# A transformer trunk on one core: an attention group's second projection wave done one projection at a time and evicted straight from PSUM, and VectorE work in the down projection tied to later instructions

## The chip, the cores and the metric

The kernel runs on one core of a Trainium2 chip. The metric is the device time of one execution in microseconds. The times come from runs of the kernel and from one execution taken by the hardware profiler. In the text PE is TensorE (matmul), DVE is VectorE, ACT is ScalarE, POOL is GpSimd, and SP is the queue from which most transfers are issued.

## The reference

A bidirectional encoder trunk of two layers on a sequence of 1024 tokens of width 1024, all in float32. Each layer has a parallel mix of four attention groups and then a squared-ReLU MLP:

```
for l in range(2):
    h = rms_norm(x, norm1_g[l])
    proj = h @ w_in[l]                      # columns of groups a, b, c, d
    y_a = mla_mixer(...)                    # latent attention, 4 heads
    y_b = diff_mixer(b_q, b_k, b_v, ...)    # differential attention, 4 heads, two softmaxes each
    y_c = swa_mixer(...)                    # +-128 window with sinks
    y_d = na_mixer(...)                     # neighbourhood attention on a 64-wide grid
    mix = concatenate([rms_norm(y_a), y_b, rms_norm(y_c), rms_norm(y_d)])
    x = x + mix @ w_out[l]
    h = rms_norm(x, norm2_g[l])
    x = x + square(relu(h @ w_up[l])) @ w_down[l]
return rms_norm(x, final_norm_g)
```

Group b's q and k get rotary position factors; its v does not.

## The kernel before

**Products in parts.** Data lies transposed: 128 features by 1024 tokens in a tile. A float32 product is made of three passes (`passes`, lines 218 to 223): each operand is split into a rounded high part and the rest, the low part, and TensorE computes high x high, high x low and low x high into one PSUM bank of 128x512. So a projection of 128 columns is 2 halves of tokens x 8 blocks of features x 3 passes = 48 matmuls. For weights, `weights` (line 202) loads a tile of four 128x128 blocks into `ws` (2 buffers), ACT rounds it into `wh`, and POOL computes the low part `wl` (tag `w`, 3 buffers of each). `split` (line 191) does the two steps. Which engine makes a low part is an argument; for activations it is mostly DVE.

**The schedule.** The program is written in an order, and a planner at build time sorts each engine's instructions by its own timing model and by priority (the order written, with offsets by `high_priority`). Tiles of a pool share buffers by tag. In the MLP TensorE's order is the written one (`manual_schedule`), the other engines' orders are planned. `issue_after(ins)` queues every instruction written inside it that runs on the engine of `ins` behind `ins` on that engine; it orders the queue and waits for nothing else.

**Start of attention** (`attention`, from line 407). PSUM has eight banks here: `mm` 2, `tr` 2, `sb` 3, `pv` 1. Group b's projections come in two waves of three: Q, K and V of the first pair of heads (wave 0), then those of the second pair (wave 1). `several` (line 231) computes a wave in six banks (`sb`, `sb`; `sb`, `tr`; `tr`, `pv`), in two rounds c over the two halves of the features; in a round all three projections take turns, so each round needs three weight tiles at a time. At the start of the second round it calls `catch_up`, which writes whatever has been put off in `self.due`. After a wave, each bank is copied by ACT into a tile `p` (line 480), and an eviction works from there:

- `ev_rope` (line 621) for Q and K, per half of the tokens: one DVE multiplication by the table `tabc`, two half-height ones by `tabs`, into two `part` tiles (3 buffers), an addition, and `emit_parts`: ACT's high part and a low part, then two transfers to memory. The addition and the low part run on `self.eng`: DVE for wave 0, POOL for wave 1.
- `ev_plain` (line 637) for V: one DVE multiplication by `rb`, and then `to_values`: a turn by four TensorE transposes into a bank, ACT's high part, DVE's low part, a transfer. For wave 0 the turn is put off in `self.due` and uses a bank of `mm`; for wave 1 it is written at once and uses `tr`.

Then `weave` interleaves the attention of group b (`attn_b`: scores into `sb`, DVE's row extreme `nm` on line 855, ACT's exponential, transposes into `tr`, products into `pv`) with a filler: the latent projections and those of group d, each through `one` (line 427): a weight pair by `wtile`, per half a bank of `mm`, `product`, `catch_up`, eviction. `attn_b` reads q, k and v back from memory (tile `stack`).

**Down projection** (`mlp_down`, line 1456). It is a Strassen-like scheme of seven block products for each of four groups j. For a group, `op(o)` loads four tiles of activations and splits them (ACT high, DVE low, tile `far`); `block` makes twelve matmuls of 128x512 with one raw weight tile, of which ACT and POOL make the parts; `add` is a DVE addition of a bank to the residual `x`. DVE also forms weight sums (tile `raw`): `s1`, and differences into `a21` and `a11`. In the written order a group has: four blocks with `op(1)`; four with `op(2)`, with each of them that column's sums; then `op(6)` and its four blocks, `op(7)`, `op(4)`, `op(5)`, `op(3)`. For j = 0 the up projection's last steps are mixed in: `finish_up[0]` with the DVE instruction kept in `self.rectified`, and everything on DVE of the second four blocks stands behind that instruction.

Of the kernel before, what the change touches and what calls it, by code (L numbers as in the profile page):

```python
# [15 lines left out]
AF = mybir.ActivationFunctionType  # L16
# [128 lines left out]
class Trunk:  # L145
# [85 lines left out]
    def several(self, srcs, xs, banks, ahead=None):  # L231

        for c in range(2):
            if c:
                self.catch_up()
            ws = ahead if ahead and c == 0 else [self.weights(s[c]) for s in srcs]
            for k in range(4):
                for w, b in zip(ws, banks):
                    for n in range(2):
                        self.passes(b[n], w[k], xs[4 * c + k], slice(n * 512, n * 512 + 512),  # L240
                                    c == 0 and k == 0, c == 1 and k == 3)
# [165 lines left out]
    def attention(self, l):  # L407
# [43 lines left out]
        with ExitStack() as stack, ExitStack() as att:  # L451
            self.ap = att.enter_context(sbuf("att"))
            with self.banks(mm=2, tr=2, sb=3, pv=1):
                with sbuf("proj", "right") as self.pp:
                    first = [w_in(t) for t in self.WAVES[0]]
                    saved = d["x"]
                    ahead = self.first
                    if l:
                        saved = self.dram.tile([8, P, S], F, tag="saved", bufs=1, name="saved")
                        for k in range(8):  # L460
                            self.keep(saved[k], self.x[k])
                        ahead = None
                    xs = self.normed(self.g1[:, l], lambda n: self.big_tile(R, n))

                    def wave():
                        return [(self.bank(a), self.bank(b)) for a, b in (("sb", "sb"), ("sb", "tr"), ("tr", "pv"))]

                    banks = wave()
                    self.several(first, xs, banks, ahead)
                    acc = self.squares(self.x, self.ap, "p", self.NP)  # L470
                    with tc.high_priority(offset=200):
                        self.spread_here(rb, self.rstd_cols(acc, DM, self.ones[:, 0:1]))
                    tabs = self.table("32", rb, nc.vector)
                    self.eng = nc.vector
                    for t in range(2):
                        for ev, b in zip(evacs_b(t), banks):
                            raw = self.ptile()
                            for n in range(2):
                                sl = slice(n * 512, n * 512 + 512)
                                nc.scalar.activation(raw[:, sl], b[n], AF.Copy)  # L480
                                ev(n, raw[:, sl])
                        if t == 0:
                            banks = wave()
                            self.several([w_in(t) for t in self.WAVES[1]], xs, banks)
                        self.eng = nc.gpsimd

                    fill = chain(self.proj_latent(l, one, xs, rb, tabs, lat, krd, rows), proj_d())
                    self.weave(chain.from_iterable(self.attn_b(l, t, qb, kb, vb, y["b"]) for t in range(2)),
                               fill, self.RB, self.LB, every=self.EV[0])
                    self.tails.append(self.mix_b(mix, y["b"], self.gsub[:, l:l + 1]))  # L490
                    fill = chain(proj_c(), self.latent_up(l, lat, rows, qa, ka, va))
                    self.weave(self.attn_d(l, qd, kd, vd, y["d"]), fill, self.RD, self.LD, every=self.EV[1])
                gout = lambda n: self.gout[n][:, l]
                self.tails.append(self.mix_group(mix, 2, y["d"], gout("na")))
                wa = stack.enter_context(sbuf("wa", "right"))
                wo = stack.enter_context(sbuf("wo", "right"))
                sums, w_out = [], d["w_out"][l]

                def groups_bd():

                    for m in range(self.EARLY):
                        x = wo.tile([P, S], F, tag="sum", bufs=self.EARLY, name="sum")
                        self.load(x, saved[m])
                        sums.append(x)
                    for k in (0, 2):
                        xs = mix[k:k + 2]
                        while None in xs:
                            yield True
                            xs = mix[k:k + 2]
                        for m, x in enumerate(sums):  # L510
                            ws = self.weights(w_out[m, 0][:, k:k + 2])
                            for n in range(2):
                                ps = self.mm_ps()
                                self.product(ps, ws, xs, n)
                                sl = slice(n * 512, n * 512 + 512)
                                self.tt(x[:, sl], ps, x[:, sl], ALU.add)
                                yield True

                fill = groups_bd()
                self.weave(self.attn_c(l, qc, kc, vc, y["c"]), fill, self.RC, end=False, every=self.EV[2])  # L520
                self.tails.append(self.mix_group(mix, 4, y["c"], gout("swa")))
                self.weave(self.attn_a(l, qa, ka, krd, va, y["a"]), fill, self.RA, self.LA, every=self.EV[3])
                self.tails.append(self.mix_group(mix, 6, y["a"], gout("mla"), nc.vector))
# [932 lines left out]
    def mlp_down(self, l, acts):  # L1456
# [4 lines left out]
        with self.banks(u=4, p=4):  # L1461
            def add(m, n, ps):
                o = self.x[m][:, N[n]]
                return self.tt(o, ps, o, ALU.add)

            for j in range(4):
# [31 lines left out]
                for m in M:  # L1498
                    a21.append(w(m + 4, 0, "c"))
                    a22.append(w(m + 4, 1, "c"))  # L1500
                with ExitStack() as behind:
                    if j == 0:
                        behind.enter_context(tc.issue_after(self.rectified.ins))
                    for m in M:
                        ps = self.bank("p")
                        self.block(ps, a12[m], b)
                        add(m, 0, ps)
                        s1.append(self.raw_weights("b"))
                        self.tt(s1[m], a21[m], a22[m], ALU.add)
                        sub(a21[m], a11[m], a21[m])  # L1510
                        sub(a11[m], s1[m], a11[m])
                if j == 1:
                    with tc.issue_after(added.ins):
                        self.finish_up[1]()
                b = op(6)
                for m in M:
                    self.block(u[m], a11[m], b, start=False)
                    add(m, 1, u[m])
                b = op(7)
                for m in M:  # L1520
                    self.block(u[m], a21[m], b, start=False)
                    add(m + 4, 1, u[m])
                    sub(a12[m], a12[m], a11[m])
                b = op(4)
                for m in M:
                    self.block(u[m], a22[m], b, start=False)
                    add(m + 4, 0, u[m])
# [136 lines left out]
```

## Time and profile before

| what | before |
|---|---|
| median of 3 runs | 2643.9 us (2641.38 to 2647.65) |
| profiled execution, its own time | 2649.87 us |
| its span | 2648.1 us |
| mean granted TensorE clock | 0.975 |
| PE busy | 2524.9 us, 95% of the span |
| DVE busy | 1950.6 us, 74% |
| ACT busy | 1443.9 us, 55% |
| POOL busy | 1134.4 us, 43% |
| instructions | 37521 |

The profiled execution is 6 us, 0.2%, above the median of the runs; its own time is 1.8 us more than its span. A row of the trace has a start, a duration in us, the engine, the line, the operation, the tiles out<-in, the shape, and in brackets how long the engine stood idle before it and what released it. Matmuls overlap, so the distance between two starts, not the duration, is what one costs. A row of the waits has the total, the times and the longest. A row of a group has the count, then busy time in us and the mean in ns, then idle time before.

### The profile page before, as it was taken

How to read it: one execution, taken by the hardware profiler on the slowest of the kernel's cores; microseconds unless marked ns; L12 is line 12 of the kernel's file. 1: busy time of each engine (PE TensorE's matmuls, PEld its weight loads, DVE VectorE, ACT ScalarE, POOL GpSimd, SP SyncE). 2: the span in 40 equal slices, each digit the busy share in tenths (PEclk: the TensorE clock that was granted, in tenths of full speed). 3: DMA queues.
4: the chain of work that ended last, by engine and by line, in shares of the span. 5: the costliest groups of instructions: out<-in, count | busy, mean ns of one | idle time of the engine just before them, and what ended most of it. 6: DMA issues, size and time to landing. Idle time of an engine off the chain costs nothing.

```text
span 2648.1 us, 37521 instructions
## 1 busy us (share of the span) xinstructions
PE 2524.9 (95%) x12320; PEld 2097.0 (79%) x12320; DVE 1950.6 (74%) x3403; ACT 1443.9 (55%) x2612; POOL 1134.4 (43%) x800
## 2 busy tenths in 40 slices
PE   8899998999999998999998999889999999989998
PEld 7678887877788887888877788777877888878886
DVE  6687767784986668887558777778749866678776
ACT  4577766673644444444426777666735444444445
POOL 2565642301055555555415657332011555555544
PEclk9889999999999999999998999899999999999999
DMA  5634598321144456544244445963221544665431
GB/s 169 183 88 130 146 268 260 101 90 50 63 167 153 153 192 225 154 150 140 99 119 145 118 133 155 281 206 90 80 72 35 193 147 155 234 194 165 131 116 64
DMA packets 191539, 385.00 MB, mean 145 GB/s; under 512 B 23712, under 2 KB 34928, under 8 KB 191344
## 3 DMA queue, kind: packets, MB, share of 16 engines
q1 hardware_dynamic: 176976, 356.90, 43.9%
q10 hardware_dynamic: 14368, 25.70, 2.8%
q8 instruction: 98, 1.61, 0.2%
q14 instruction: 97, 0.79, 0.1%
HBM read 261.20 MB, written 121.32 MB: 144 GB/s over the span
## 4 chain that ended last, share of the span: by engine, by line
PE 74%; DVE 10%; DMA 6%; ACT 4%; issue 3%; POOL 2%; SPq 1%; DVEq 0%; POOLq 0%; ACTq 0%
PE u L221 9%; PE u L223 9%; PE u L222 8%; PE p L223 5%; PE p L221 5%; PE p L222 5%; PE mm L221 5%; PE mm L222 5%; PE mm L223 5%; PE sb L853 3%; PE tr L889 2%; DVE p L855 2%; DVE part L189 2%; DMA bias<-in_bias 2%; ACT p L858 1%
## 5 line engine op out<-in xcount | busy, mean ns | idle before, releaser
L189 POOL TENSOR_TENSOR wl<-raw,wh 128x512 fp32r<-128x512 f32 x424 | 611.9, 1444 | 688.9 <-ACT wh L195 671.4
L195 ACT ACTIVATE wh<-raw 128x512 fp32r<-128x512 f32 x448 | 282.2, 630 | 559.0 <-PE u L222 302.0
L189 POOL TENSOR_TENSOR wl<-ws,wh 128x512 fp32r<-128x512 f32 (+1 forms) x120 | 151.9, 1267 | 420.9 <-ACT wh L195 411.4
L223 PE MATMUL u<-far,wl 128*128 128x512 f32 x768 | 300.7, 392 | 12.7 <-POOL wl L189 12.7
L221 PE MATMUL u<-far,wh 128*128 128x512 f32 x768 | 300.2, 391 | 2.3 <-ACT ev L1292 2.3
L222 PE MATMUL u<-far,wh 128*128 128x512 f32 x768 | 300.2, 391 | 0.0
L189 DVE TENSOR_TENSOR raw<-raw 128x512 f32<-128x512 f32 x256 | 227.0, 892 | 80.8 <-DMA raw<-in_w_up 45.1
L189 DVE TENSOR_TENSOR ptl<-tr,pth 128x512 fp32r<-128x512 f32 (+2 forms) x384 | 238.8, 629 | 61.2 <-ACT pth L195 59.6
L858 ACT ACTIVATE p<-p,nm 128x1024 f32<-128x1024 f32 x192 | 220.4, 1148 | 78.2 <-DVE nm L855 76.1
L195 ACT ACTIVATE pth<-tr 128x512 fp32r<-128x512 f32 (+2 forms) x384 | 206.9, 548 | 100.5 <-PE tr L889 68.4
L223 PE MATMUL p<-far,wl 128*128 128x512 f32 (+1 forms) x648 | 251.2, 388 | 3.0 <-DVE wl L189 3.0
L221 PE MATMUL p<-far,wh 128*128 128x512 f32 (+1 forms) x648 | 251.2, 388 | 0.0
L222 PE MATMUL p<-far,wh 128*128 128x512 f32 (+1 forms) x648 | 250.8, 387 | 0.0
L853 PE MATMUL sb<-stack 96*128 96x512 f32 x640 | 220.0, 426 | 15.7 <-DVE nm L855 15.1
L189 DVE TENSOR_TENSOR far<-act,far 128x512 fp32r<-128x512 f32 x224 | 202.2, 933 | 14.9 <-ACT far L195 14.9
L189 POOL TENSOR_TENSOR p<-p 128x1024 f32<-128x1024 f32 x64 | 154.6, 2416 | 104.1 <-ACT p L941 97.7
L223 PEld LDWEIGHTS u<-far,wl 128*128 128x128 f32 x768 | 145.1, 189 | 43.7 <-POOL wl L189 13.6
L221 PEld LDWEIGHTS u<-far,wh 128*128 128x128 f32 x768 | 145.0, 189 | 33.2 <-ACT ev L1292 3.1
L222 PEld LDWEIGHTS u<-far,wh 128*128 128x128 f32 x768 | 144.9, 189 | 30.8 <-DVE far L189 0.8
L889 PE MATMUL tr<-ident,p 128*128 128x128 f32 x1024 | 162.1, 279 | 7.5 <-DVE ptl L189 6.2
L221 PE MATMUL mm<-xh,wh 128*128 128x512 f32 x416 | 165.9, 399 | 2.1 <-DVE part L189 1.9
L855 DVE CUSTOM_DVE_ANT_0 p<-sb,zero 128x512 f32<-128x512 f32 x192 | 129.2, 685 | 52.3 <-PE sb L853 17.3
(256 smaller groups left out, 6148.4 us busy)
## 6 DMA issues: line engine op xcount, KB each, us to landing
act<-acts SPq DMA_DIRECT2D x224, 256.0 KB, 2.8
raw<-in_w_up SPq DMA_DIRECT2D x128, 256.0 KB, 2.7
acts<-ev SPq DMA_DIRECT2D x128, 256.0 KB, 2.2
raw<-in_w_down SPq DMA_DIRECT2D x128, 256.0 KB, 2.7
acts<-ev ACTq DMA_DIRECT2D x96, 256.0 KB, 2.5
ws<-in_w_in SPq DMA_DIRECT2D x76, 256.0 KB, 2.7
rz<-drows SPq DMA_DIRECT2D x40, 256.0 KB, 3.6
stack<-kd SPq DMA_DIRECT2D x32, 256.0 KB, 5.6
```

What stands on the lines that cost most here:

```text
L189: return (eng or self.nc.vector).tensor_tensor(out=out, in0=a, in1=b, op=op)
L195: self.rounded = nc.scalar.activation(hi, src, AF.Copy)
L221: mm(ps, w[0], x[0][:, sl], start=start, stop=False)
L222: mm(ps, w[0], x[1][:, sl], start=False, stop=False)
L223: mm(ps, w[1], x[0][:, sl], start=False, stop=stop)
L853: self.nc.tensor.matmul(ps, q[:, qt * P:(qt + 1) * P], k[:, sl], start=i == 0, stop=i == len(passes) - 1)
L855: self.nc.vector.tensor_tensor_reduce(out=p[:, sl], in0=ps, in1=self.zero[:, 0:1].bitcast(F).broadcast_to([P, 512]), scale=-scale, scalar= ...
L858: self.nc.scalar.activation(p, p, AF.Exp, bias=nm[:, 1:2], scale=-1.0, accum_out=z)
L889: nc.tensor.transpose(t[:, k * 256 + i * P:k * 256 + (i + 1) * P], p[:, (j * 2 + k) * P:(j * 2 + k + 1) * P], self.ident)
```

## The change

In `several` the call of `catch_up` between the rounds goes. In `attention` the evictions of wave 0 read the banks themselves, with no ACT copy; then wave 1 is done as `one` does it, projection by projection: both weight tiles, then per half of the tokens a bank (`mm` for Q, `sb` for K, `mm` for V), the product, `catch_up` and the eviction from the bank.

In `mlp_down` `op(6)` is written ahead of the second four blocks instead of behind them, in all four groups j. For j = 0 its DVE work stands behind the last addition of the first four blocks (`added`), and so does the DVE work of columns 2 and 3 of the second four; that of columns 0 and 1 stays behind `self.rectified`. For j = 0 the DVE work of `op(7)` and `op(4)` stands behind the last addition of the second four blocks (`passed`).

```diff
     def several(self, srcs, xs, banks, ahead=None):
 
         for c in range(2):
-            if c:
-                self.catch_up()
             ws = ahead if ahead and c == 0 else [self.weights(s[c]) for s in srcs]
...
                     self.eng = nc.vector
-                    for t in range(2):
-                        for ev, b in zip(evacs_b(t), banks):
-                            raw = self.ptile()
-                            for n in range(2):
-                                sl = slice(n * 512, n * 512 + 512)
-                                nc.scalar.activation(raw[:, sl], b[n], AF.Copy)
-                                ev(n, raw[:, sl])
-                        if t == 0:
-                            banks = wave()
-                            self.several([w_in(t) for t in self.WAVES[1]], xs, banks)
-                        self.eng = nc.gpsimd
+                    for ev, b in zip(evacs_b(0), banks):
+                        for n in range(2):
+                            ev(n, b[n])
+                    self.eng = nc.gpsimd
+                    for t, ev, tag in zip(self.WAVES[1], evacs_b(1), ("mm", "sb", "mm")):
+                        ws = self.wtile(w_in(t))
+                        for n in range(2):
+                            ps = self.bank(tag)
+                            self.product(ps, ws, xs, n)
+                            self.catch_up()
+                            ev(n, ps)
...
-                with ExitStack() as behind:
-                    if j == 0:
-                        behind.enter_context(tc.issue_after(self.rectified.ins))
-                    for m in M:
+                behind = lambda ins: tc.issue_after(ins.ins) if j == 0 else ExitStack()
+                c = b
+                with behind(added):
+                    b = op(6)
+                for m in M:
+                    with behind(self.rectified if m < 2 else added):
                         ps = self.bank("p")
-                        self.block(ps, a12[m], b)
-                        add(m, 0, ps)
+                        self.block(ps, a12[m], c)
+                        passed = add(m, 0, ps)
                         s1.append(self.raw_weights("b"))
                         self.tt(s1[m], a21[m], a22[m], ALU.add)
                         sub(a21[m], a11[m], a21[m])
...
-                b = op(6)
                 for m in M:
                     self.block(u[m], a11[m], b, start=False)
                     add(m, 1, u[m])
-                b = op(7)
+                with behind(passed):
+                    b = op(7)
                 for m in M:
                     self.block(u[m], a21[m], b, start=False)
                     add(m + 4, 1, u[m])
                     sub(a12[m], a12[m], a11[m])
-                b = op(4)
+                with behind(passed):
+                    b = op(4)
                 for m in M:
                     self.block(u[m], a22[m], b, start=False)
                     add(m + 4, 0, u[m])
```

## The prediction, made before the run

> **What bounds the kernel now.** I read the page's busy times first, then TensorE's waits stage by stage, and last the rows in order of time around the two places that the diff touches.
>
> ```profile
> span 2648.1 us, 37521 instructions
> PE 2524.9 (95%) x12320; PEld 2097.0 (79%) x12320; DVE 1950.6 (74%) x3403; ACT 1443.9 (55%) x2612; POOL 1134.4 (43%) x800
> ```
>
> TensorE is the bound, and the diff neither adds nor removes a matmul. So the change is worth what it takes from, or adds to, the time in which TensorE stands still or runs slowly. TensorE's waits, in the windows 0 to 130, 1000 to 1330, 1340 to 1470 and 2290 to 2649 us:
>
> ```profile
> PE sb L853 <- DVE nm L855: 5.3, 2, 3.0
> ...
> PE u L223 <- POOL wl L189: 6.1, 1, 6.1
> ...
> PE sb L853 <- DVE nm L855: 4.4, 2, 3.3
> PE tr L221 <- ACT wh L195: 3.9, 1, 3.9
> ...
> PE u L223 <- POOL wl L189: 6.7, 1, 6.7
> ```
>
> The start of each layer's attention and the start of each layer's down projection each hold a few long stalls; the 6.1 is the only wait of the down projection of layer 0 that the answer lists. Layer 0's attention start, in TensorE's order of time:
>
> ```profile
> 45.71 0.39 PE L221 MATMUL sb<-xh,wh 128*128 128x512 f32 x1
> 62.04 1.03 PE L679 MATMUL mm<-ident,part 128*128 128x128 f32 x8
> 68.38 0.39 PE L223 MATMUL tr<-xh,wl 128*128 128x512 f32 x1
> 72.18 0.50 PE L221 MATMUL tr<-xh,wh 128*128 128x512 f32 x1 [3.40 <-ACT wh L195]
> 73.04 0.63 PE L222 MATMUL pv<-xl,wh 128*128 128x512 f32 x1
> 75.60 0.63 PE L221 MATMUL tr<-xh,wh 128*128 128x512 f32 x1
> 84.38 0.39 PE L223 MATMUL pv<-xh,wl 128*128 128x512 f32 x1
> 97.03 0.39 PE L223 MATMUL mm<-xh,wl 128*128 128x512 f32 x1
> 113.54 0.63 PE L221 MATMUL mm<-xh,wh 128*128 128x512 f32 x1
> 116.52 0.63 PE L222 MATMUL mm<-xl,wh 128*128 128x512 f32 x1
> ```
>
> Wave 1 runs from 45.71 to 84.38. Its first 72 matmuls take 16.33 us, 0.227 each. There are two losses. **The weight switch:** nothing starts between 68.38 and 72.18 (3.6 us beyond one step), and then 7 matmuls step by 0.427 instead of 0.227 (73.04 to 75.60 is six steps), 1.4 us more: 5.0 us. **After the wave:** the latent projection's two halves end at 97.03 and its next product starts at 113.54. In those 16.3 us TensorE has this to do:
>
> ```profile
> L853 PE MATMUL sb<-stack 96*128 96x512 f32 x9 | 6.1, 733 | 5.5 <-DVE nm L855 5.3
> L679 PE MATMUL tr<-ident,part 128*128 128x128 f32 x8 | 2.2, 431 | 1.2 <-DVE part L189 1.2
> ```
>
> Nine 512-column scores at 0.23 are 2.1 us; the transposes and some single-column sums add about 1.1: 3.2 us of work, 13.1 lost, and 8 slow steps from 113.54 add 1.6: 14.7 us. VectorE at the same place:
>
> ```profile
> 43.85 3.42 DVE L189 TENSOR_TENSOR part<-p,tabs 64x512 f32<-64x512 f32 x2
> 58.88 1.29 DVE L189 TENSOR_TENSOR part<-p,rb 128x512 f32<-128x512 f32 x2
> 64.86 0.69 DVE L189 TENSOR_TENSOR both<-mm,both 128x512 fp32r<-128x512 f32 x1 [0.81 <-ACT both L683]
> 82.04 0.69 DVE L189 TENSOR_TENSOR part<-p,tabc 128x512 f32<-128x512 f32 x1 [16.49 <-ACT p L480]
> ...
> 107.92 0.68 DVE L189 TENSOR_TENSOR part<-mm,rb 128x512 f32<-128x512 f32 x1
> ```
>
> VectorE stands idle for 16.5 us while TensorE works through wave 1, because all six of the wave's banks finish together. Then the whole eviction of wave 1 meets the first softmaxes, from 82.04 to 108. The latent product's bank is emptied only at 107.92, behind it.
>
> **The change part by part. 1. Projection by projection.** Each of wave 1's three products is 48 matmuls, 10.9 us, and is evicted while the next runs. What VectorE does for wave 1 between 82 and 113 us now:
>
> ```profile
> L189 DVE TENSOR_TENSOR part<-p,tabs 64x512 f32<-64x512 f32 x8 | 10.0, 1250 | 2.8 <-POOL part L189 2.7
> L189 DVE TENSOR_TENSOR part<-p,tabc 128x512 f32<-128x512 f32 x4 | 3.8, 952 | 16.9 <-ACT p L480 16.5 <-POOL both L189 0.4
> L189 DVE TENSOR_TENSOR part<-p,rb 128x512 f32<-128x512 f32 x2 | 2.8, 1408 | 0.0
> ```
>
> That is 16.6 us and some 3.1 idle for POOL. All but the last half of V moves ahead of 82 us, into VectorE's 16.5 idle ones, and with it the POOL part of the ropes. The loss after the wave is 14.7 in layer 0. In layer 1 the same hole is:
>
> ```profile
> 1407.26 0.39 PE L223 MATMUL mm<-xh,wl 128*128 128x512 f32 x1
> 1422.17 0.63 PE L221 MATMUL mm<-xh,wh 128*128 128x512 f32 x1
> ```
>
> 14.7 us from matmul to matmul less about 3 of work, plus 1 of slow steps: 12.7. Together 27.4. Bounds: 0 (the first softmax groups are a chain of their own, which no eviction shortens) and -27.4 (16.6 + 3.1 us leave VectorE's path, more than is lost). I take half, -13.7: the softmax chain has nothing ready before its first group, so the hole closes only in part.
>
> The switch stall goes as well: a product uses both its weight halves one behind the other, and the third weight buffer lets the next be loaded ahead. The SP queue issues the same six weight loads, in the order Q, Q, K, K, V, V instead of Q, K, V twice, so fewer of them stand behind the loads of the attention's stacks. That removes 5.0 in layer 0 and 5.3 in layer 1 (3.9 and as many slow steps): -10.3.
>
> It adds a wait. V's two transposes of wave 0 now stand behind Q's first half, in the same two `mm` banks that Q's second half needs, and the tiles of a tag are handed out in the order of the program. Q's first half ends at 45.71 + 24 x 0.227 = 51.2, and V's rows are there at 58.88 to 60.2. Behind the waiting Q stand its second half and V; K does not, as it is in `sb`, and with one weight loaded its two halves hold 24 matmuls, 5.4 us, so TensorE is covered to 56.6. The second bank comes free at about 60, after the first turned half's low part. Ends: 0 (K's other weight is there too, and covers it) and 65.55 - 51.2 = 14.4 plus 1.5 of slow clock, if nothing covers it. I take 3 a layer, near the covered end: +6.
>
> **2. No copies.** 24 ACT copies of this kind go.
>
> ```profile
> L480 ACT ACTIVATE p<-sb x12: 583/590/600, 42.5 to 1393.2; 128x512 f32<-128x512 f32 x12
> L189 DVE TENSOR_TENSOR part<-p,tabs x16: 684/687/1761, 43.8 to 101.7; 64x512 f32<-64x512 f32 x16
> ```
>
> ACT is no bound there (only the first copy is on the path, 0.6 us a wave): 0. VectorE's reads cost the same from a bank as from SBUF, 0.68 us at 107.92 (`mm`) against 0.69 at 82.04 (`p`), both of 128x512: 0. [...] The other way, at 43.85 two half-height operations take 3.42 us where twice the median of 687 ns is 1.37: both inputs are in SBUF and POOL is at work. With one input in a bank that loss, 2.0 us, may go; it is inside the bounds.
>
> **3. Down.** In layer 0, around the 6.1:
>
> ```profile
> 1012.86 0.39 PE L222 MATMUL u<-far,wh 128*128 128x512 f32 x1
> 1019.30 0.80 PE L223 MATMUL u<-far,wl 128*128 128x512 f32 x1 [6.05 <-POOL wl L189]
> 1024.59 0.63 PE L223 MATMUL p<-far,wl 128*128 128x512 f32 x1
> L189 POOL TENSOR_TENSOR wl<-raw,wh x424: 1271/1297/8277, 720.4 to 2624.4; 128x512 fp32r<-128x512 f32 x142
> 1011.43 7.82 POOL L189 TENSOR_TENSOR wl<-raw,wh 128x512 fp32r<-128x512 f32 x1 [4.69 <-ACT wh L195]
> 1018.04 0.69 DVE L189 TENSOR_TENSOR x<-u,x 128x512 f32<-128x512 f32 x1
> L189 DVE TENSOR_TENSOR raw<-raw 128x512 f32<-128x512 f32 x10 | 7.1, 732 | 0.0
> L189 DVE TENSOR_TENSOR far<-act,far 128x512 fp32r<-128x512 f32 x8 | 5.3, 682 | 0.0
> ```
>
> (three of TensorE's rows, POOL's low parts with their least, median and longest time in ns, one row each of POOL and VectorE, and VectorE's groups between 1006 and 1018.03.) One low part of a weight takes POOL 7.82 us instead of 1.3. It ends 1.3 us after 1018.04, when VectorE turns for the first time from an unbroken row of operations on SBUF alone, ten weight sums and eight low parts among them, to one that reads a bank. [...]
>
> The loss: 6.2 to the matmul, and 13 slow steps of 0.2 to 1024.59: 9.0 us; as much in layer 1, 18 in all. After the change op(6)'s low parts and two of the four columns' sums wait for the last addition of the first four blocks, and op(7) and op(4) for the last addition of the second four. The row breaks after six sums (3.6 us), before POOL's 11.43; POOL ends at 12.7 and TensorE needs it at 13.09. What comes late next: op(6) is needed two groups of four blocks after, at 1015.8 + 10.9 = 1026.7 without the stall; four low parts and six sums at 0.6 from 1016 end at 1022. ACT's first parts of op(6) and the SP loads, four more ahead of the loop, are issued as early as now and hidden by the same 10.9. For j = 1 to 3 only op(6) moves ahead; TensorE has no wait there now: 0. Bounds 0 (the new row of lows and sums holds POOL as long) and -18; I take -16.5.
>
> **Sum**, on the profiled execution's 2649.87: -10.3 + 6 - 13.7 - 16.5 = -34.5, 2615.4. That execution is 6 above the median, so the median 2643.9 becomes 2609.
>
> **The rivals.** *A, all of it comes back:* -10.3 - 27.4 - 18 = -55.7, 2588. For: VectorE's idle 16.5. Against: the new wait. 12 in 100. *B, the start pays nothing:* the wait for a bank eats the switch, and the softmax chain fills the hole: -16.5, 2627. For: the scores wait for `nm`, a softmax result. 16 in 100. *C, the row of VectorE work only moves behind the addition and holds POOL there:* -18, 2626. Against: additions from banks stand in between. 10 in 100. *D, slower:* Q's second half waits with nothing beside it, because the order written at build time places K behind it: 16 us a layer against 5.0 removed, +22, the eviction is as late as before, so nothing of the hole closes, and V's banks come late again, 3 a layer: +28 - 16.5, 2655. It decides from 13 us a layer (5.1 removed and 8.2 from down). Against: K is in banks of its own. 9 in 100. *E, neither part does what it says:* 2644, 8 in 100. The forecast: 45 in 100.
>
> **How the numbers follow.** A change within 0.2%, 5.3 us, can hardly be told from none here. Faster: forecast, A, B, C, 83; E and a little of D, same, 9; slower 8. The likeliest's own range is 2596 to 2622. Leaving out half of A below and E and D above, 2590 to 2636.
>
> **What would show it.** Right: no wait on `wh` in wave 1, `part<-mm` and `part<-sb` rows of VectorE between 60 and 82, the hole between latent products under 8 us; in down POOL's longest `wl` under 3 us and no wait of `u L223`. Wrong: TensorE waiting between 51 and 65 us for a bank of `mm`, or a POOL `wl` of 6 us and more behind the additions.

## The result, and the profile after

| | before | after |
|---|---|---|
| median of 6 runs | 2644.83 us (2640.34 to 2651.1) | 2624.43 us (2623.08 to 2625.5) |
| ratio to before | | 0.9922, 95% interval 0.9908 to 0.9936 |
| profiled execution | 2649.87 us | 2624.3 us |
| its span | 2648.1 us | 2622.5 us |

The change made the kernel 20.4 us faster, 0.78%. The forecast was 2609 with a range of 2590 to 2636: the sign is right, and the time lies in the range, 2 us above that of the likeliest case (2596 to 2622): 14 of the forecast 34.5 us are missing. The two profiled spans differ by 25.6 us, but some 5 us of that belong to the one execution of before that was profiled, which was about 5 us above its median. Of the experiments below, e2 and e4 each had one execution of about twice the time (5892 and 4970 us), which the ratios leave out.

The page's busy times after:

```profile
span 2622.5 us, 37463 instructions
PE 2512.9 (96%) x12320; PEld 2087.0 (80%) x12320; DVE 1922.8 (73%) x3403; ACT 1427.7 (54%) x2588; POOL 1120.9 (43%) x800
```

The 24 copies are gone from ACT (2612 instructions to 2588). TensorE has the same 12320 matmuls in 25.6 us less span.

**The attention start.** Code lines behind the diff have moved by two (L853 is now L851, L679 is L677, L855 is L853). TensorE's waits in the windows 0 to 130 and 1340 to 1470 us:

```profile
PE sb L851 <- DVE part L189: 3.8, 1, 3.8
PE mm L677 <- DVE part L189: 1.3, 1, 1.3
PE sb L223 <- POOL wl L189: 0.5, 1, 0.5
...
PE sb L851 <- DVE part L189: 5.0, 1, 5.0
PE mm L677 <- DVE part L189: 1.3, 1, 1.3
```

The wait for `wh` in the middle of wave 1 is gone, and so are the long waits for `nm`. In their place stand a short wait for the turn in a bank of `mm`, as forecast, and one of 3.8 and 5.0 us at the second score, which I had not forecast. Layer 0 in TensorE's order of time:

```profile
58.95 0.66 PE L677 MATMUL mm<-ident,part 128*128 128x128 f32 x4 [1.34 <-DVE part L189]
...
83.53 0.39 PE L851 MATMUL sb<-stack 96*128 96x512 f32 x1
87.76 0.50 PE L851 MATMUL sb<-stack 96*128 96x512 f32 x1 [3.84 <-DVE part L189]
...
103.62 0.48 PE L223 MATMUL mm<-xh,wl 128*128 128x512 f32 x1
...
106.19 0.40 PE L221 MATMUL mm<-xh,wh 128*128 128x512 f32 x1
```

From the last matmul of the latent projection's two halves to its next product it is now 2.6 us (103.62 to 106.19); it was 16.5 (97.03 to 113.54). What holds the score at 87.76, in the rows of ACT, POOL and DVE:

```profile
83.09 0.63 ACT L195 ACTIVATE wh<-ws 128x512 fp32r<-128x512 f32 x1 [7.03 <-DMA ws<-in_w_in]
...
83.80 1.26 POOL L189 TENSOR_TENSOR wl<-ws,wh 128x512 fp32r<-128x512 f32 x1 [6.37 <-ACT wh L195]
85.02 1.26 POOL L189 TENSOR_TENSOR part<-part 128x512 f32<-128x512 f32 x1
...
86.31 1.39 DVE L189 TENSOR_TENSOR part<-sb,tabs 64x512 f32<-64x512 f32 x2 [5.72 <-POOL part L189]
```

Read from the bottom: DVE cannot go on with K's eviction (which would free a bank of `sb` for the score) before POOL's addition has been done, as the three `part` tiles are in use. POOL's addition stands in its queue behind a low part `wl`, that waits for ACT's `wh`, and that for a transfer. But these are the weights of the first latent projection, whose product starts at 89.86. The transfer was issued at 77.05, into a stretch in which the DMA engines are full (a row of the busy times by stretches: its window and length, then busy time and count of PE, of PE's weight loads, of DVE, ACT and POOL, the granted clock, the DMA share and GB/s):

```profile
75.00:80.00 5.00, 5.00 (x24) 4.13 (x23) 2.60 (x6) 0.63 (x1) 1.69 (x2) 1.00 0.98 338
```

**The down projection.** Its long stall has not gone but moved. TensorE, DVE, POOL and ACT in layer 0:

```profile
1027.37 0.50 PE L221 MATMUL u<-far,wh 128*128 128x512 f32 x1 [1.45 <-ACT wh L195]
...
1031.36 0.80 PE L223 MATMUL u<-far,wl 128*128 128x512 f32 x1 [3.26 <-POOL wl L189]
...
1024.08 0.68 DVE L189 TENSOR_TENSOR x<-p,x 128x512 f32<-128x512 f32 x1
1024.68 5.49 DVE L189 TENSOR_TENSOR far<-act,far 128x512 fp32r<-128x512 f32 x9
...
1027.39 6.85 POOL L189 TENSOR_TENSOR wl<-raw,wh 128x512 fp32r<-128x512 f32 x3 [6.18 <-ACT wh L195]
...
1026.17 0.63 ACT L195 ACTIVATE far<-act 128x512 fp32r<-128x512 f32 x1 [7.06 <-DMA act<-acts]
1026.70 0.61 ACT L195 ACTIVATE wh<-raw 128x512 fp32r<-128x512 f32 x1
...
SPq L160 <- DVE far L189: 7.6, 9, 3.6
```

(The last row is one of SP's waits from 1015 to 1040 us.) The addition at 1024.08 is the one that the diff calls `passed`. Behind it DVE runs nine low parts in one unbroken row: those that were tied behind it, and one of op(5), which was not. POOL's low parts meet that row. And ACT stands 7.06 us in front of an activation that has not been loaded, with the weights' `wh` behind it in its queue. That load was issued at 1023.59, after SP had waited 3.6 us for a low part of DVE: a load needs one of ten tiles (`piece`, tag `raw`), and a tile is in use until its low part has been made. By the order of the loads, the roundings and the low parts it is op(5)'s third tile, while the tied low parts of op(7) and op(4) held eight of the ten.

How much a layer loses there I count in one way for all kernels below: in the 50 us that begin 30 us after the up projection's last matmul into the tile `q` (980.91 us before, layer 0), 50 less 0.2268 us for each matmul of 128x512 that starts. 0.2268 us is the step of the first 72 matmuls of wave 1 before. One matmul more or less at the edge makes 0.2 us. Layer 0 and layer 1: before 9.2 and 8.3; after 8.0 and 7.4.

### The profile page after: what moved, and what is told of

Its sections match the earlier page's. It is cut to its first block, busy times and chain, and to the rows that moved or that the text cites. A ratio compares the mean times of both kernels' runs of the same rounds, so it can differ in the third digit from the quotient of the medians.

```text
span 2622.5 us, 37463 instructions
## 1 busy us (share of the span) xinstructions
PE 2512.9 (96%) x12320; PEld 2087.0 (80%) x12320; DVE 1922.8 (73%) x3403; ACT 1427.7 (54%) x2588; POOL 1120.9 (43%) x800
## 4 chain that ended last, share of the span: by engine, by line
PE 67%; DVE 8%; issue 5%; ACT 4%; DMA 3%; POOL 1%; SPq 0%; DVEq 0%; POOLq 0%; ACTq 0%
PE u L223 9%; PE u L221 9%; PE u L222 9%; PE p L223 5%; PE p L222 5%; PE p L221 5%; PE mm L221 4%; PE mm L222 4%; PE mm L223 4%; PE sb L851 2%; DVE p L853 2%; PE tr L887 2%; ACT p L856 2%; DVE ptl L189 1%; DVE part L189 1%
## 5 line engine op out<-in xcount | busy, mean ns | idle before, releaser
L189 POOL TENSOR_TENSOR wl<-raw,wh 128x512 fp32r<-128x512 f32 x424 | 603.8, 1426 | 695.0 <-ACT wh L195 679.1
L851 PE MATMUL sb<-stack 96*128 96x512 f32 x640 | 218.6, 422 | 14.2 <-DVE part L189 8.9
L221 PE MATMUL mm<-xh,wh 128*128 128x512 f32 x480 | 191.0, 398 | 4.6 <-DVE part L189 4.6
L223 PE MATMUL mm<-xh,wl 128*128 128x512 f32 x480 | 190.1, 396 | 0.0
L222 PE MATMUL mm<-xl,wh 128*128 128x512 f32 x480 | 189.2, 394 | 0.0
```

The source lines that it names most:

```text
L189: return (eng or self.nc.vector).tensor_tensor(out=out, in0=a, in1=b, op=op)
L221: mm(ps, w[0], x[0][:, sl], start=start, stop=False)
L222: mm(ps, w[0], x[1][:, sl], start=False, stop=False)
L223: mm(ps, w[1], x[0][:, sl], start=False, stop=stop)
L851: self.nc.tensor.matmul(ps, q[:, qt * P:(qt + 1) * P], k[:, sl], start=i == 0, stop=i == len(passes) - 1)
```

## The experiments

All times below are medians; ratios are to runs of the kernel before on the same chip, with 95% intervals. "Loss" is the down projection's loss just defined, layer 0 and layer 1.

| run | median us | ratio to before | interval | loss in down |
|---|---|---|---|---|
| e1_start_only | 2627.08 | 0.9945 | 0.9927 to 0.9964 | 8.5, 8.7 |
| e2_down_only | 2633.18 | 0.9966 | 0.9953 to 0.9979 | 3.1, 6.5 |
| e3_copies_back | 2625.08 | 0.9938 | 0.9921 to 0.9955 | 8.5, 7.8 |
| e4_wave1_vector | 2652.01 | 1.0034 | 1.0023 to 1.0044 | 6.9, 7.4 |
| e5_untied | 2621.59 | 0.9922 | 0.9906 to 0.9939 | 6.2, 6.2 |
| e8_rows_split | 2620.98 | 0.9921 | 0.9904 to 0.9937 | 5.1, 6.0 |
| e11_wl_vector | 2623.83 | 0.9927 | 0.9909 to 0.9946 | 5.5, 5.5 |
| e12_latent_later | 2620.92 | 0.9925 | 0.9906 to 0.9945 | 5.8, 6.5 |
| e13_after_rounding | 2613.98 | 0.9881 | 0.9866 to 0.9896 | 0.8, 0.0 |
| e14_both | 2615.81 | 0.9898 | 0.9880 to 0.9916 | 0.1, 0.1 |
| e15_sums_only | 2623.69 | 0.9918 | 0.9905 to 0.9931 | 6.7, 5.5 |
| e16_after_again | 2624.23 | 0.9923 | 0.9910 to 0.9936 | 6.7, 7.1 |

**e1 and e2: the two parts alone.** e1 is the changed kernel with the function `mlp_down` of before; e2 is the kernel before with the changed `mlp_down`.

```diff
 # e1: after, but
-                with behind(added):
-                    b = op(6)
...
+                with ExitStack() as behind:
+                    if j == 0:
+                        behind.enter_context(tc.issue_after(self.rectified.ins))
...
 # e2: before, but
+                with behind(added):
+                    b = op(6)
...
```

> The change's attention start, with the down stage as it was before. Theory: the two attention starts carry the whole gain, about 8.7 us in layer 0 and 13.5 in layer 1, so the time is some 22 us below before (ratio 0.9916, near 2623) and within 3 us of the changed kernel. Rival: the down stage pays what was forecast for it (16.5 us over both layers) when it is seen alone, so this kernel lands near 2636, only 7 us below before.

> The change's down stage alone, with the attention start as it was before. Theory: the two ties (the sums behind the addition, op(7) and op(4) behind the last partial addition) take away the 6.05 us stall of layer 0 and bring 1.45 + 3.26 us and a slow stretch instead, so a layer gains about 1 us and the time is 2 us below before (ratio 0.9992). Rival: the stage pays 16.5 us alone (ratio 0.9938, near 2628) and lost it in the changed kernel only because its start had moved against the weight transfers.

The start alone gave 14.5 us (10 to 19), the down part alone 9.0 (6 to 12). Both of my numbers missed: the start is worth less than 22, since the trace of before that I had compared with held the 5 us of that one execution; and the down part is worth more than 2 where it stands alone. From the first matmul of wave 1 to the first of the up projection, layer 0 and layer 1, the trace of before takes 641.7 and 646.0 us, that of e2, whose start is the same, 640.7 and 639.9, and that of e1 633.4 and 632.9. Between e2 and e1 that is 14.3 us in both layers, which is what the times of e1 give. The old stall of the down part is there in e1, the new ones in layer 1 of e2, while layer 0 of e2 has a single wait (one row each, e1 and two of e2):

```profile
1011.65 0.80 PE L223 MATMUL u<-far,wl 128*128 128x512 f32 x1 [6.66 <-POOL wl L189]
```

```profile
1036.67 0.50 PE L223 MATMUL u<-far,wl 128*128 128x512 f32 x1 [2.96 <-POOL wl L189]
...
2338.45 0.50 PE L223 MATMUL u<-far,wl 128*128 128x512 f32 x1 [3.15 <-POOL wl L189]
```

So one and the same order loses 3.1 or 6.5 us, and over the twelve layers that were traced with it (after, e2, e3, e4, e12, e16) 3.1 to 8.5, 6.8 in the mean, against 8.3 to 9.2, 8.7 in the mean, over the four with the order of before. The part is worth about 2 us a layer by the mean of the traces, and up to 9 in all by the times of e2, whose own trace lost 7.9 us less than that of before.

**e3: the copies back.** The free banks and the order projection by projection stay.

```diff
+                        raw = self.ptile()
...
-                            ev(n, b[n])
...
+                            nc.scalar.activation(raw[:, sl], b[n], AF.Copy)
+                            ev(n, raw[:, sl])
...
-                            ev(n, ps)
+                            nc.scalar.activation(raw[:, sl], ps, AF.Copy)
+                            ev(n, raw[:, sl])
```

> The changed kernel with the 24 ScalarE copies put back (bank to a tile in the state buffer, then VectorE or GpSimd reads the tile), projection by projection as changed. Theory: it is the free banks and the projection by projection order that pay; the copies are beside TensorE and the time stays within 4 us of the changed kernel (ratio to before 0.992 to 0.9935). Rival: the PSUM source is what breaks the unbroken row of VectorE additions that kept GpSimd out (the longest read 7.82 us for one operation before); with the copies back the latent products wait again and 8 to 14 us of the gain go (near 2634, ratio 0.996).

0.9938 is 1.6 thousandths (4 us) from the changed kernel, whose 0.9922 lies inside e3's interval; the rival's 0.996 lies just outside. The traces decide it: from wave 1 to the up projection e3 takes 1266.5 us in both layers together, the changed kernel 1264.6 and 1266.3 (its second trace, e16), e1 1266.3 and e2 1280.6. The copies are hidden, as the theory says, and the gain of the start is that of the order and the banks; how much belongs to which of these two was not tested. In this trace DVE's reads of the state buffer (SBUF) took longer beside POOL: of the same `tabc` products two take 1.62 and 1.76 us, begun while POOL was at work, where one with POOL idle takes 0.69. It lies beside TensorE. The trace of before has it too: 1.74 us at 97.91, with POOL at work from 97.84, against 0.69 at 91.84, with POOL idle. The rows of e3:

```profile
60.92 1.62 DVE L189 TENSOR_TENSOR part<-p,tabc 128x512 f32<-128x512 f32 x1
...
74.06 0.69 DVE L189 TENSOR_TENSOR part<-p,tabc 128x512 f32<-128x512 f32 x1 [7.32 <-ACT p L488]
...
83.90 1.76 DVE L189 TENSOR_TENSOR part<-p,tabc 128x512 f32<-128x512 f32 x1 [2.83 <-POOL both L189]
```

**e4: wave 1's additions and low parts on DVE.**

```diff
-                    self.eng = nc.gpsimd
                     for t, ev, tag in zip(self.WAVES[1], evacs_b(1), ("mm", "sb", "mm")):
...
                             ev(n, ps)
+                    self.eng = nc.gpsimd
```

> The changed kernel with the second wave's evictions and rotations on VectorE instead of GpSimd for their additions. Theory: the new stalls of the first scores (3.84 us in layer 0, 5.03 in layer 1, ended by a VectorE operation that waits for a GpSimd addition behind a late low part of the latent weights) go, so the time is 5 to 9 us below the changed kernel (near 2617, ratio 0.9897). Rival: the late transfer of the weights itself is the limit; the latent product that follows waits instead and the time stays within 2 us of the changed kernel. Second rival: the rows fill VectorE and the turned banks come free later, 2 to 6 us slower than the changed kernel.

A clear miss: 9 us slower than the kernel before, where the changed kernel is 20 faster. The stall stayed, on another engine: the latent weights' `wh` now stands ahead of ACT's rounding of K in ACT's queue (rows of ACT, DVE and TensorE, layer 0).

```profile
81.57 0.63 ACT L195 ACTIVATE wh<-ws 128x512 fp32r<-128x512 f32 x1 [13.07 <-DMA ws<-in_w_in]
82.11 0.61 ACT L195 ACTIVATE both<-part 128x512 fp32r<-128x512 f32 x1
...
82.75 1.40 DVE L189 TENSOR_TENSOR both<-part,both 128x512 fp32r<-128x512 f32 x1 [6.49 <-ACT both L195]
...
86.81 0.80 PE L851 MATMUL sb<-stack 96*128 96x512 f32 x1 [4.17 <-DVE part L189]
```

And the planner, with POOL's queue emptier, moved other work: in layer 1 the tables of the next group stand ahead of two softmax operations on POOL and wait for their own transfer, with 8.86 us of TensorE behind them (rows of POOL and TensorE).

```profile
1463.97 2.34 POOL L189 TENSOR_TENSOR tabc<-tabc,rb 128x1024 f32<-128x1024 f32 x1 [4.56 <-DMA tabc<-in_c]
...
1469.12 4.67 POOL L189 TENSOR_TENSOR p<-p 128x1024 f32<-128x1024 f32 x2
...
1471.52 1.54 PE L887 MATMUL tr<-ident,p 128*128 128x128 f32 x6 [8.86 <-POOL p L189]
```

That is one wait of several that grew; I did not take the difference apart further.

**e5, e8 and e11: which of two causes makes the new stall of the down projection.** Two theories were left after the first runs. One: the row of nine holds POOL out. Two: low parts that are tied late keep the activation tiles in use, so that the next loads, ACT's roundings of them and the `wh` queued behind these come late. e5 lets the low parts go where they went before; e8 ties them later still, but in shorter rows; e11 takes POOL out of it.

```diff
 # e5
-                with behind(passed):
-                    b = op(7)
+                b = op(7)
...
-                with behind(passed):
-                    b = op(4)
+                b = op(4)
 # e8: later is the last addition of the op(6) group, last7 that of the op(7) group
-                    add(m, 1, u[m])
+                    later = add(m, 1, u[m])
...
-                    add(m + 4, 1, u[m])
+                    last7 = add(m + 4, 1, u[m])
...
-                with behind(passed):
+                with behind(later):
                     b = op(4)
...
-                b = op(5)
+                with behind(last7):
+                    b = op(5)
 # e11: for the op(6) group's four blocks
+                was = self.lows
+                if j == 0:
+                    self.lows = nc.vector
                 for m in M:
                     self.block(u[m], a11[m], b, start=False)
                     add(m, 1, u[m])
+                self.lows = was
```

> The changed kernel without the ties of op(7) and op(4) to the last partial addition; the sums and op(6) stay tied. Theory: the gathered row of low parts (nine VectorE instructions, 5.49 us, in which GpSimd's low parts of the weights take up to 3.9 us each) and the late roundings of the activations behind it make the 1.45 and 3.26 us stalls of the down stage; with the low parts spread again both go, a layer loses under 3 us there instead of 7 to 8, and the time is some 9 us below the changed kernel (ratio to before 0.9888). Rival: the low parts then stand ahead of the first addition, as before the change, and a 6 us stall comes back in their place: within 3 us of the changed kernel.

> The changed kernel with the low parts of op(4) tied behind the last addition of the op(6) group and those of op(5) behind the last one of the op(7) group, so that the row of nine becomes rows of four to six, as late as before or later. Theory one (the unbroken row holds GpSimd out): the 3.26 us stall and the slow stretch behind it go, 5 us a layer, ratio 0.9885. Theory two (the late low parts hold the activation tiles, so that their next loads, the roundings queued behind them on ScalarE, and the weights' roundings come late): the 1.45 us stall stays or grows to 3 us, and the gain is under 2 us a layer, ratio 0.991 to 0.994.

> The changed kernel with the low parts of the op(6) group's four weight blocks of the first quarter on VectorE instead of GpSimd. Theory one (GpSimd is held out by the row): the four low parts take 0.6 us each in VectorE's own row, the 3.26 us stall shrinks below 1 us with the slow stretch, 5 us a layer, ratio 0.9885. Theory two (ScalarE's late roundings set it): the low part waits for the same rounding, VectorE waits with it in its order, the stalls stay near 1.5 and 3 us and the time is that of the changed kernel (0.992).

None of the three moved the time by what its first theory says; by the trace each took one cause away and kept the other. In e5 no wait for `wh` is left, but POOL is held as long as in the changed kernel, 3.91 us, here beside a row of five sums and low parts between the additions at 1021.66 and 1025.27 (POOL's low parts from 990 to 1050 us with their least, median and longest time in ns; then TensorE's row):

```profile
L189 POOL TENSOR_TENSOR wl<-raw,wh x19: 1287/1301/3907, 992.4 to 1047.6; 128x512 fp32r<-128x512 f32 x19
```

```profile
1026.53 0.50 PE L223 MATMUL u<-far,wl 128*128 128x512 f32 x1 [2.81 <-POOL wl L189]
```

In e8 no low part of POOL takes longer than 1.75 us and its wait shrinks to 0.62, but the wait for `wh` has grown from 1.45 to 2.38 us (the same two views, with ACT's rows):

```profile
L189 POOL TENSOR_TENSOR wl<-raw,wh x21: 1278/1302/1752, 988.7 to 1049.4; 128x512 fp32r<-128x512 f32 x21
```

```profile
1032.51 0.50 PE L221 MATMUL u<-far,wh 128*128 128x512 f32 x1 [2.38 <-ACT wh L195]
...
1033.87 0.80 PE L223 MATMUL u<-far,wl 128*128 128x512 f32 x1 [0.62 <-POOL wl L189]
...
1028.67 0.63 ACT L195 ACTIVATE far<-act 128x512 fp32r<-128x512 f32 x1 [6.20 <-DMA act<-acts]
1031.31 0.63 ACT L195 ACTIVATE far<-act 128x512 fp32r<-128x512 f32 x1 [2.01 <-DMA act<-acts]
1031.85 1.13 ACT L195 ACTIVATE wh<-raw 128x512 fp32r<-128x512 f32 x2
```

In e11 the low part stands in DVE's own queue behind a row of six, and starts when ACT's late `wh` (from 1026.59, 0.61 us) is there; TensorE waits as long as for POOL:

```profile
1023.59 3.68 DVE L189 TENSOR_TENSOR far<-act,far 128x512 fp32r<-128x512 f32 x6
1027.19 0.68 DVE L189 TENSOR_TENSOR wl<-raw,wh 128x512 fp32r<-128x512 f32 x1
...
1027.93 0.50 PE L223 MATMUL u<-far,wl 128*128 128x512 f32 x1 [3.29 <-DVE wl L189]
```

So each theory has its wait in the traces, and neither alone is enough: with one cause removed the other still costs 5 to 6 us a layer.

**e12: the first latent weights' split later.** The load stays where it is; ACT's roundings of the two tiles stand behind ACT's rounding of K's first half.

```diff
-        self.split(wh, wl, st, eng=self.nc.gpsimd)
+        with self.tc.issue_after(self.hold.pop().ins) if self.hold else ExitStack():
+            self.split(wh, wl, st, eng=self.nc.gpsimd)
...
                             ev(n, ps)
+                            if tag == "sb" and n == 0:
+                                held = self.rounded
+                    self.hold = [held] * 2
```

> The changed kernel with the split of the first latent weights (both halves, ScalarE's rounding and GpSimd's low part) tied behind ScalarE's rounding of the second K projection's first half. Theory: the 3.84 us (layer 0) and 5.03 us (layer 1) stalls of the first scores come from those two splits, which stand ahead of the rotation's addition on GpSimd and wait for a late load; out of the way, the stall falls below 1.5 us in both layers with the slow steps behind it, 6 to 9 us, ratio 0.989. Rival: the latent products that fill the gaps between scores come late instead, at about 92 us and later, and give the gain back: within 3 us of the changed kernel.

The scores' wait for `part` is gone in both layers, so its chain was read rightly, but the scores behind wait instead (TensorE's waits from 0 to 120 us; lines have moved by five):

```profile
PE sb L856 <- DVE nm L858: 2.5, 2, 2.1
PE mm L682 <- DVE part L190: 1.3, 1, 1.3
```

The ratio, 0.9925, is that of the changed kernel: the rival's number, though not its place.

**e13, e14, e15, e16: both causes at once, and what is left.** e13 ties op(7) behind ACT's second weight rounding of the op(6) group, so that the group's first two `wh` go ahead of op(7)'s activations on ACT and op(7)'s low parts on DVE are free again, and has the later ties of e8. e14 is e13 with e12, and the turns of wave 0's V in `tr`. e15 is e5 with op(6) untied as well. e16 is the changed kernel again.

```diff
 # e13, beside the later ties of e8
                 for m in M:
                     self.block(u[m], a11[m], b, start=False)
+                    if m == 1:
+                        split = self.rounded
...
-                with behind(passed):
+                with behind(split):
                     b = op(7)
 # e14, beside e12 and e13
-                    self.ev_plain(rb, self.to_values(vb[2 * t:2 * t + 2], "tr" if t else "mm"))]
+                    self.ev_plain(rb, self.to_values(vb[2 * t:2 * t + 2], "tr"))]
 # e15, beside e5
-                with behind(added):
-                    b = op(6)
+                b = op(6)
```

> The changed kernel with op(7) tied behind the second weight rounding of the op(6) group (instead of the last partial addition), op(4) behind the last addition of the op(6) group and op(5) behind that of the op(7) group. Theory: two causes stand in one chain, activation roundings that wait for late loads ahead of the weights' roundings on ScalarE (about 2 us of stall) and the row of nine low parts that holds GpSimd out (about 3 us, with the slow stretch); this order takes both away, the loss of the down stage's first 50 us falls from 7 to 8 us to under 3 us a layer, some 9 to 10 us in all, ratio to before 0.9885. Rival: the low parts of op(7) then come late for their own group and a wait of 2 to 4 us appears at its first block; within 3 us of the changed kernel.

> The same order of the down stage, together with the later split of the first latent weights and the turns of both V projections of the first wave in the free bank. Theory: the gains add: 9 to 10 us from the down stage and 4 to 7 us from the attention starts, ratio 0.986 to 0.9875. Rival: the attention starts are held by the transfers, whose engines are busy 98 to 100 percent of the time from 65 to 90 us, so that taking one wait away moves it to the next scores: only the down stage's gain is seen, ratio 0.9885.

> The changed kernel with only the weight sums tied in the down stage; op(6), op(7) and op(4) all free. Theory: the low parts spread again and load early, which takes the two new stalls away, but they stand ahead of the sums in VectorE's order, and the stall of the kernel before comes back at 3 to 6 us a layer: ratio 0.992 to 0.994. Rival: the tie of the sums is all that was needed; the loss of the stage is under 3 us a layer and the ratio 0.9885.

> The changed kernel unchanged, for a second trace and as the reference of this call. Expected 0.9922 of before; if the stalls of the down stage are set by how loads land, its loss there differs from the first trace (8.1 and 7.4 us in the two layers) by some us, and if by the order alone, by less than 0.5 us.

e13 did what its theory says: 2613.98 us against 2624.23 for the changed kernel on the same chip, with intervals that do not meet. Its profile at the same place (busy times of the 50 us, of before and then of e13; e13's low parts on POOL; and its rows of DVE and ACT with the only wait of TensorE there):

```profile
1010.90:1060.90 50.00, 43.95 (x182) 35.85 (x181) 40.45 (x51) 19.85 (x33) 29.31 (x17) 0.93 0.55 170
```

```profile
1005.70:1055.70 50.00, 49.38 (x219) 40.45 (x218) 46.40 (x59) 23.98 (x42) 26.88 (x19) 1.00 0.61 196
```

```profile
L189 POOL TENSOR_TENSOR wl<-raw,wh x22: 1281/1486/1749, 990.6 to 1049.8; 128x512 fp32r<-128x512 f32 x22
```

```profile
1024.52 3.58 DVE L189 TENSOR_TENSOR far<-act,far 128x512 fp32r<-128x512 f32 x4
...
1018.79 5.30 ACT L195 ACTIVATE far<-act 128x512 fp32r<-128x512 f32 x10
1024.00 0.62 ACT L195 ACTIVATE wh<-raw 128x512 fp32r<-128x512 f32 x1
...
1030.37 0.51 PE L223 MATMUL u<-far,wl 128*128 128x512 f32 x1 [0.62 <-POOL wl L189]
```

219 matmuls in the stretch instead of 182, at a granted clock of 1.00 instead of 0.93; four low parts in a row ahead of `passed`, and none between it and the additions of op(6)'s group, where there had been nine; ten roundings of activations together on ACT from loads issued ahead of them, and then `wh`, at 1024.00, with no wait. In layer 1 there is no wait at all.

e14 shows the same in the down projection (0.1 and 0.1) and the shortest profiled span of all, 2611.2, but its runs gave 0.9898: its rival's case, the start's further gain not shown. e15 brought the stall of before back at 3.64 and 3.66 us, as its theory says. But it ran at 0.9918, and e5, which has the tie of op(6), at 0.9922: neither the tie of op(6) nor those of op(7) and op(4) show a worth of their own in the times, since each takes one stall away and leaves or brings another. e16 lost 6.7 and 7.1 against 8.0 and 7.4 in the first trace: the order makes the stall, and it varies by a microsecond from one execution to another; that the loads do this is not shown. e13 beats both kernels.

## Why the prediction was right in sign and too large

I compare by the same kind of count (time beyond 0.2268 us for each 512 columns, so that sums of one column count as almost nothing), layer 0 and layer 1 in turn. From wave 1's start to the score behind it (after the change, the one that waits) TensorE lost 5.8 and 7.2 us before and 7.2 and 8.4 after; in the 36 us from that score on 15.8 and 14.5 before, 6.3 and 6.4 after.

- *The switch, -10.3:* right. No wait for `wh` is left in wave 1.
- *The wait for a bank of `mm`, +6:* right in kind and too large. It is 1.34 us a layer, with 0.5 for a low part behind it. Wave 1 by itself lost 3.2 us in each layer where it had lost 5.8 and 7.2, which is 6.7 less, so the new waits in it gave back some 3.6 of the 10.3 instead of 6. That is near the covered end of the bound.
- *Not in the list:* the score's wait, 3.84 and 5.03, 9.2 with what came with it. With it the stretch lost 2.5 us more than before, where my two terms had 4.3 less. I had counted the transfers of the new order as fewer ahead of the weights, but not looked at what stands behind a late one in the queues of ACT and POOL.
- *The hole after the wave, -13.7:* right in kind and too small: -9.5 and -8.1, -17.5 together, 58% of what was there instead of the half that I took. Between the latent products it closes to 2.6 us in both layers, under the 8 that I named.
- *Copies 0, reads of banks 0:* right, by e3; `part<-mm,tabc` takes 0.69 us (after, at 60.20), as `part<-p,tabc` did (before, at 82.04).
- *Down, -16.5:* this is the step that failed: the traces show -2.1 and -3.7 in all (after and its second trace), and the part alone gave 9.0. That there was so much to be had was right: 17.5 before, of which e13 took 16.7. What failed were two sentences. "ACT's first parts ... and the SP loads ... are issued as early as now and hidden": not all were, because a tied low part keeps its activation tile in use, and ACT then stood 7.06 us in front of a load with the weights behind it. And "the row breaks after six sums": it did, but the low parts which I had moved behind `passed` formed a row of nine there. That is rival C's mechanism, to which I gave 10 in 100 because "additions from banks stand in between"; none stands inside these nine. As beside the old row, where one low part took POOL 7.82 us, POOL was slow beside the new one: its low part took 3.91 us in it at the longest, and 1.75 where e8 broke it up.

Two readings in the part on down were off, with no effect on this. Six sums and eight low parts stand in the unbroken row ahead of 1018.04, since `ev<-p,ev` at 1009.02 reads a bank; the other four sums come before it. And 6.2 and 13 times 0.2 make 8.8, not 9.0.

Together: 2.5 - 17.5 = -15.0 for the start where I had -18.0, near the 14.5 of e1, and about -3 for down where I had -16.5: -18, where the runs give -20.4 with an interval of 17 to 24. That the start came so near to its sum is partly luck: a wait that I had not seen (+9.2) was made up for by a smaller loss in wave 1 and by a hole that closed further. That the time lies in my range is owed to the width of the range, not to the down term. Of the signs that I had named as right those of the start came, and those of down did not; of those named as wrong, the wait for a bank of `mm` came, at 58.95 and small. Rivals B and C had named about this time; B's reason is wrong (the start is what paid), C's is the right one for the down part, and only half of it, as the queue of ACT is the other. Rival D, Q's second half waiting uncovered, did not come: the wait is 1.34.

## What to carry to other kernels

When an instruction is tied later, ask what it holds: here a low part held its input tile, the tile held a load, the load a rounding, and the rounding a weight that was ready. Look at where tied work gathers, as a new row is as long as what was tied to one place, and order each engine's queue separately, since a tie on one engine leaves the others as they were. Where two causes stand at one wait, taking one away shows little; only both together showed the 10 us.

## What the runs showed of the hardware that was not expected

- The cost of a wait beyond itself is uneven. After 2.96 us (e2) TensorE went on at 0.23 a step at once; after 3.26 us, with a wait of 1.45 (in e16 1.23) four microseconds earlier, 12 steps followed at 0.43 in one trace and 7 in the other (e16) of the same kernel (layer 0). What decides it stays open.
- DVE took longer beside POOL as well: while POOL made three low parts (1018.64 to 1023.34), three weight sums of DVE took 4.60 us, 1.53 each, where the three at 1021.52 of e13, with POOL idle, took 1.88 together (a row of e16):

```profile
1019.28 4.60 DVE L189 TENSOR_TENSOR raw<-raw 128x512 f32<-128x512 f32 x3
```

- One order of instructions lost 3.1 to 8.5 us at the same place in twelve traced layers: a single trace of such a stall is no price.
